# Hybrid decoder layer on one core: the mixer's sums of squares taken with the squares as the stationary operand, and kept on chip until the group's root

## The chip, the cores and the metric

The kernel runs on one core of one Trainium2 chip. The metric is the device time of one execution in microseconds (us), lower is better. A core has five engines that run their own instruction streams and meet through semaphores: TensorE (PE in the profile, with its weight loads shown apart as PEld), VectorE (DVE), ScalarE (ACT), GpSimd (POOL) and SyncE (SP), which here only issues DMAs.

## The reference

A layer norm of x (1024 rows of 1024), one large input projection, two token mixers in parallel, a gated merge, an output projection and a second layer norm. The change lies in the state-space mixer's gated group norm:

```
def gated_group_rmsnorm(y, z, g):
    h = (y * jax.nn.silu(z)).astype(jnp.float32)
    hg = h.reshape(*h.shape[:-1], SSM_GROUPS, -1)
    hg = hg * lax.rsqrt(jnp.mean(jnp.square(hg), axis=-1, keepdims=True) + RMS_EPS)
    return (hg.reshape(h.shape) * g).astype(y.dtype)
```

There are 4 groups of 512 channels and 1024 rows of sequence, so the norm needs 4 x 1024 means of squares, and of each its reciprocal root.

## The kernel before

The input projection is cut into 44 pairs of column tiles of the weights (`pairs`). A pair is seven products (`item_p`, lines 945 to 947 issue the matmuls: 4 blocks of k, each with 3 matmuls of 512 columns). Products of the pairs follow one another on PE without a break. ACT copies every weight block into a rounded form (`whip`, line 276), DVE forms the rest (`wlop`, line 106), POOL forms sums of weight blocks (`s`, `raw_a`: lines 236 to 250). Tiles `pU`, `p`, `oa`, `ob` are the products' PSUM banks and their sums in SBUF.

Between the products the state-space mixer is worked off in small stages (`micro`, one list of stages for each of 4 groups x 8 chunks of 128 rows of the sequence = 32 chunks, numbered n = 8g + c). One entry of the list is issued after each item of the projection, so the order on every engine is the order in which the program is written (`pin`). A chunk ends so: `s_gate_z` forms y * silu(z), `s_square` squares it (ACT, tile `z`, 128 channels x 4 x 128 rows), `s_fold` adds the four channel blocks on POOL, and `s_sum` lets PE add the 128 channels. PE takes two operands: the stationary one, which is loaded into the array first (a row LDWEIGHTS on PEld), and the moving one, which is streamed through it (a row MATMUL). A matmul of f32 is two such passes; a transpose is one.

Before the change `s_sum` has a column of ones as stationary operand (128 x 1) and the squares as moving operand (128 x 128); the result is one row of 128 sums on one partition. ACT scales the row into SBUF (tile `row`) and issues a DMA into DRAM (`ssq_d`). After a group's eighth chunk (`group_rstd`) POOL loads the 1024 sums back as 128 x 8 (`ms`), ACT and DVE form the reciprocal root (`rsqrt`: tiles `rqa`, `rqb`, `rr`), and POOL writes it to `rst_d`. From there `prep_y` (line 784) reads it much later as rows spread over all partitions.

The DMAs that POOL issues are written by POOL itself; those of SP and ACT go through a queue of their own engine.

Of the kernel before, what the change touches and what calls it, by code (L numbers as in the profile page):

```python
# [19 lines left out]
F32 = mybir.dt.float32  # L20
F32R = mybir.dt.float32r
AF = mybir.ActivationFunctionType
# [3 lines left out]
P = 128  # L26
L = 1024
# [3 lines left out]
NCH = 8  # L31
H = 32
G = 4
# [12 lines left out]
def trunk_kernel(ctx: ExitStack, tc: tile.TileContext, x, w_in, w_dt, w_a, w_s, w_o, par, con,  # L46
                 dt_bias, a_log, ln_in_g, ln_in_b, ln_g, ln_b, out):
    nc = tc.nc
    V, S, Gp, PE, SP = nc.vector, nc.scalar, nc.gpsimd, nc.tensor, nc.sync
# [7 lines left out]
    bc_d = [tc.dram_tile([P, 2, L], F32, name=f"bc_d{g}") for g in range(G)]  # L57
    cum_d = tc.dram_tile([H, L], F32, name="cum_d")
    ecum_d = tc.dram_tile([H, L], F32, name="ecum_d")
    ssq_d = [tc.dram_tile([1, L], F32, name=f"ssq_d{g}") for g in range(G)]  # L60
    rst_d = [tc.dram_tile([1, L], F32, name=f"rst_d{g}") for g in range(G)]

    cst = ctx.enter_context(tc.tile_pool(name="cst", bufs=1))
# [3 lines left out]
    ident, upper, slow, ones = (con_t[:, i * P:(i + 1) * P] for i in range(4))  # L67
# [17 lines left out]
    def rsqrt(pool, r, v, n, tag):  # L85

        ve = pool.tile([P, n], F32, tag=tag + "a", name=tag + "a")
        q = pool.tile([P, n], F32, tag=tag + "b", name=tag + "b")
        S.activation(q, v, AF.Sqrt, bias=eps_t, scale=1.0)
        V.tensor_scalar(ve, v, EPS, -0.5, ALU.add, ALU.mult)  # L90
        V.reciprocal(r, q)
        if n == 1:
            V.scalar_tensor_tensor(q, r, ve, r, ALU.mult, ALU.mult)
        else:
            V.tensor_tensor(q, r, r, ALU.mult)
            V.tensor_tensor(q, q, ve, ALU.mult)
        V.scalar_tensor_tensor(r, q, 1.5, r, ALU.add, ALU.mult)
# [55 lines left out]
    def bank(tag, name):  # L153
        return pa.tile([P, HALF], F32, tag=tag, name=name, bufs={"U": 2, "yy": 2}.get(tag, 1))
# [414 lines left out]
    sd = {}  # L569
    XT, ZS, BC, EM, YT, XD, XW, CB, BS, ST = ({} for _ in range(10))  # L570

    def srows(g, c):
        return slice(c * P, (c + 1) * P)
# [131 lines left out]
    def s_store(n):  # L705
        g, c = divmod(n, NCH)
        SP.dma_start(gat_d[g][:, :, srows(g, c)], YT[n])

    def s_sum(n):
        g, c = divmod(n, NCH)  # L710
        ps = bank("tr", f"trs{n}")
        PE.matmul(ps[0:1, 256:384], lhsT=ones[:, 0:1], rhs=ZS[n][:, 0, :], start=True, stop=True)
        row = sd["p"].tile([1, P], F32, tag="row", name=f"row{n}", bufs=1)
        S.activation(row, ps[0:1, 256:384], AF.Copy, scale=1.0 / 512.0)
        S.dma_start(ssq_d[g][:, srows(g, c)], row)
        if c == NCH - 1:
            group_rstd(g)

    def group_rstd(g):
        ms = cst.tile([P, NCH], F32, tag="ms", name=f"ms{g}")  # L720
        Gp.dma_start(ms, ssq_d[g].squeeze(0).rearrange("(p c) -> p c", c=NCH))
        r = cst.tile([P, NCH], F32, tag="rr", name=f"rr{g}")
        rsqrt(cst, r, ms, NCH, "rq")
        Gp.dma_start(rst_d[g].squeeze(0).rearrange("(p c) -> p c", c=NCH), r)

    NS = G * NCH
    micro = []
# [13 lines left out]
    for n in range(NS):  # L741
        stage((s_main, n), (s_decay, n + 1, 0), (s_load_z, n))
        stage((s_rows, n), (s_decay, n + 1, 1), (s_load, n + 2))
        stage((s_gate, n))
        stage((s_turn, n + 1, 0), (s_gate_z, n), (s_load_y, n + 1))
        stage((s_turn, n + 1, 1), (s_square, n), (s_state, n), (s_load_x, n + 2))
        stage((s_mask, n + 1), (s_weigh, n + 1), (s_fold, n))
        stage((s_sum, n), (s_store, n))
# [427 lines left out]
```

## Time and profile before

| what | value |
|---|---|
| median of 3 runs | 1457.02 us (1455.95 to 1457.52) |
| the profiled execution | 1455.73 us, its span 1454.0 us |
| mean granted clock of TensorE | 0.989 of full speed |
| busy: PE, PEld, DVE, ACT, POOL | 96%, 76%, 70%, 49%, 33% of the span |
| DMA | 217.02 MB, mean 149 GB/s |

The span runs from the first to the last instruction of the profile, 1.7 us less than the time of that execution. PE is the engine that is nearly always busy; but a share over the whole span is an average, and what a change in one place is worth is read there: by the starts of successive rows on PE, and by what ended each wait.

### The profile page before, as it was taken

To read this page: it belongs to the slowest core of one execution; us is meant where nothing else is said; L and a number is where in the kernel's file an instruction comes from. 1 tells how busy PE (TensorE), PEld (TensorE's weight loads), DVE (VectorE), ACT (ScalarE), POOL (GpSimd) and SP (SyncE) were. 2 spreads that over 40 slices of the span, in tenths; PEclk is the share of its full clock that TensorE was granted. 3 is DMA by queue.
4 is the path that set the end of the run, shared out by engine and by line. 5 is a ranking of instruction groups with operands and counts; after the bars stand their busy time and mean duration, and the time that the engine had idled before them with its cause. 6 is when DMAs were issued, how large, how long until landed. Compare 5 with 4: busy or idle time off the path is not lost.

```text
span 1454.0 us, 18639 instructions
## 1 busy us (share of the span) xinstructions
PE 1396.3 (96%) x6522; PEld 1102.6 (76%) x6522; DVE 1022.1 (70%) x1495; ACT 716.0 (49%) x1243; POOL 481.0 (33%) x374
## 2 busy tenths in 40 slices
PE   6999999999999999999999999999899999959997
PEld 4677878787777878777878878787678888847786
DVE  7957878877788787787887585776534338778763
ACT  3664556555665655575645656555621233112321
POOL 4012334535244444335453344444000004331054
PEclk9999999999999999999999999999999999989999
DMA  6022354454454454454734545544547736567331
GB/s 231 16 109 80 112 144 128 137 159 133 142 130 136 138 155 123 137 131 135 172 118 134 161 125 150 151 124 138 218 162 242 232 118 218 213 212 288 131 127 62
DMA packets 171901, 217.02 MB, mean 149 GB/s; under 512 B 11520, under 2 KB 116896, under 8 KB 171808
## 3 DMA queue, kind: packets, MB, share of 16 engines
q1 hardware_dynamic: 162128, 181.80, 42.2%
q10 hardware_dynamic: 8272, 29.81, 5.2%
q0 software_dynamic: 1408, 4.23, 0.7%
q8 instruction: 51, 0.84, 0.2%
q14 instruction: 42, 0.34, 0.1%
HBM read 160.97 MB, written 54.82 MB: 148 GB/s over the span
## 4 chain that ended last, share of the span: by engine, by line
PE 80%; DVE 10%; DMA 5%; ACT 3%; issue 2%; ACTq 0%; SPq 0%; POOL 0%; POOLq 0%; DVEq 0%
PE p L945 10%; PE p L947 10%; PE p L946 10%; PE pU L947 8%; PE pU L945 8%; PE pU L946 8%; DMA yg<-yag_d 3%; PE ya L659 2%; PE p_ws L800 2%; PE p_ws L802 2%; PE p_ws L801 2%; PE p_wa L802 2%; PE p_wa L801 2%; PE p_wa L800 2%; PE st L664 2%
## 5 line engine op out<-in xcount | busy, mean ns | idle before, releaser
L106 DVE TENSOR_TENSOR wlop<-raw_a,whip 128x512 fp32r<-128x512 f32 x210 | 180.8, 861 | 171.4 <-ACT whip L276 66.7
L945 PE MATMUL p<-b,whip 128*128 128x512 f32 x352 | 144.0, 410 | 4.3 <-DVE ob L954 4.3
L945 PE MATMUL pU<-t,whip 128*128 128x512 f32 x352 | 144.7, 412 | 3.0 <-ACT oa L980 3.0
L276 ACT ACTIVATE whip<-raw_a 128x512 fp32r<-128x512 f32 x210 | 127.6, 622 | 36.9 <-issue 10.5
L945 PE MATMUL p<-t,whip 128*128 128x512 f32 x352 | 141.8, 403 | 1.5 <-DVE oa L954 1.5
L947 PE MATMUL p<-t,wlop 128*128 128x512 f32 x352 | 139.2, 395 | 1.5 <-DVE wlop L106 1.5
L946 PE MATMUL p<-b,whip 128*128 128x512 f32 x352 | 139.9, 398 | 0.0
L947 PE MATMUL p<-b,wlop 128*128 128x512 f32 x352 | 139.7, 397 | 0.0
L947 PE MATMUL pU<-t,wlop 128*128 128x512 f32 x352 | 139.0, 396 | 0.5 <-DVE wlop L106 0.4
L946 PE MATMUL p<-t,whip 128*128 128x512 f32 x352 | 138.9, 395 | 0.0
L946 PE MATMUL pU<-t,whip 128*128 128x512 f32 x352 | 138.9, 395 | 0.0
L644 POOL TENSOR_TENSOR xw<-xd,dte_t 128x256 f32<-128x256 f32 x56 | 47.0, 840 | 259.0 <-DVE xd L630 259.0
L802 PE MATMUL p_ws<-y,wlos 128*128 128x512 f32 x256 | 104.3, 408 | 12.4 <-DVE wlos L106 12.4
L801 PE MATMUL p_ws<-y,whis 128*128 128x512 f32 x256 | 103.9, 406 | 5.2 <-DVE y L106 5.2
L800 PE MATMUL p_ws<-y,whis 128*128 128x512 f32 x256 | 103.6, 405 | 0.0
L236 POOL TENSOR_TENSOR s<-raw_a,raw_a 128x512 f32<-128x512 f32 x42 | 69.5, 1654 | 85.1 <-DVE wlop L106 74.0
L250 POOL TENSOR_TENSOR raw_a<-raw_a,s 128x512 f32<-128x512 f32 x42 | 66.0, 1572 | 95.4 <-issue 87.4
L863 POOL TENSOR_TENSOR rs<-rs,ag 128x1024 f32<-128x1024 f32 x8 | 19.5, 2444 | 231.4 <-ACT rs L862 231.4
L945 PEld LDWEIGHTS p<-b,whip 128*128 128x128 f32 x352 | 66.8, 190 | 27.4 <-issue 8.8
L106 DVE TENSOR_TENSOR wlop<-s,whip 128x512 fp32r<-128x512 f32 x84 | 80.1, 966 | 9.4 <-PE p L947 6.3
L610 ACT ACTIVATE em<-em,cum_t 128x128 f32<-128x128 f32 x256 | 81.3, 390 | 7.3 <-ACT ob L554 4.4
L945 PEld LDWEIGHTS pU<-t,whip 128*128 128x128 f32 x352 | 66.1, 188 | 20.0 <-ACT oa L980 4.3
(223 smaller groups left out, 3353.7 us busy)
## 6 DMA issues: line engine op xcount, KB each, us to landing
raw_a<-in_w_in_dram SPq DMA_DIRECT2D x168, 256.0 KB
em<-cum_d SPq DMA_DIRECT2D x64, 256.0 KB
xg_d<-cv ACTq DMA_DIRECT2D x16, 512.0 KB
xT<-xg_d SPq DMA_DIRECT2D x32, 256.0 KB
z<-zs_d SPq DMA_DIRECT2D x32, 256.0 KB
gat_d<-y SPq DMA_DIRECT2D x32, 256.0 KB
rb<-rst_d SPq DMA_DIRECT2D x16, 512.0 KB
gt<-gat_d SPq DMA_DIRECT2D x16, 512.0 KB
```

Of the source, the lines that this page charges most:

```text
L106: return eng.tensor_tensor(lo, full, hi.bitcast(F32), ALU.subtract)
L236: Gp.tensor_tensor(s1, r["a21"], r["a22"], ALU.add)
L250: Gp.tensor_tensor(a12, a12, s1s[p]["s2"], ALU.subtract)
L276: S.activation(flat(hi), src, AF.Copy)
L610: S.activation(em[:, h, :], em[:, h, :], AF.Relu, bias=cum_t[:, 8 * g + 4 * i + h, c:c + 1], scale=-1.0)
L644: Gp.tensor_tensor(xw, XD[n, i], dte_t[:, hs, c].unsqueeze(2).to_broadcast([P, HG, HD]), ALU.mult)
L800: PE.matmul(ps, lhsT=hi[:, k, :], rhs=u[:, 0, :], start=start, stop=False)
L801: PE.matmul(ps, lhsT=hi[:, k, :], rhs=u[:, 1, :], start=False, stop=False)
L802: PE.matmul(ps, lhsT=lo[:, k, :], rhs=u[:, 0, :], start=False, stop=stop)
L945: PE.matmul(ps, lhsT=hi[:, k, :], rhs=u[:, 0, :], start=first, stop=False, skip_group_check=True)
L946: PE.matmul(ps, lhsT=hi[:, k, :], rhs=u[:, 1, :], start=False, stop=False, skip_group_check=True)
L947: PE.matmul(ps, lhsT=lo[:, k, :], rhs=u[:, 0, :], start=False, stop=(k == 3), skip_group_check=True)
```

## The change

`s_sum` swaps the operands: the squares become the stationary operand (128 x 128), one column of ones the moving one (128 x 1), and the 128 sums come out as a column, one on each partition. ACT scales that column straight into column c of a tile `ms` of 128 x 8. The row, its DMA into DRAM and the load back are gone. The root is formed on `ms` as before, and POOL writes it to `rst_d`. As the element for partition p and chunk c now belongs at position c * 128 + p of the DRAM row, where it was p * 8 + c, the write is of single elements instead of 8 adjoining ones.

```diff
-    ssq_d = [tc.dram_tile([1, L], F32, name=f"ssq_d{g}") for g in range(G)]
...
+    MS = {}
+
     def s_sum(n):
+
         g, c = divmod(n, NCH)
+        if c == 0:
+            MS[g] = cst.tile([P, NCH], F32, tag="ms", name=f"ms{g}")
         ps = bank("tr", f"trs{n}")
-        PE.matmul(ps[0:1, 256:384], lhsT=ones[:, 0:1], rhs=ZS[n][:, 0, :], start=True, stop=True)
-        row = sd["p"].tile([1, P], F32, tag="row", name=f"row{n}", bufs=1)
-        S.activation(row, ps[0:1, 256:384], AF.Copy, scale=1.0 / 512.0)
-        S.dma_start(ssq_d[g][:, srows(g, c)], row)
+        PE.matmul(ps[:, 256:257], lhsT=ZS[n][:, 0, :], rhs=ones[:, 0:1], start=True, stop=True)
+        S.activation(MS[g][:, c:c + 1], ps[:, 256:257], AF.Copy, scale=1.0 / 512.0)
         if c == NCH - 1:
-            group_rstd(g)
-
-    def group_rstd(g):
-        ms = cst.tile([P, NCH], F32, tag="ms", name=f"ms{g}")
-        Gp.dma_start(ms, ssq_d[g].squeeze(0).rearrange("(p c) -> p c", c=NCH))
-        r = cst.tile([P, NCH], F32, tag="rr", name=f"rr{g}")
-        rsqrt(cst, r, ms, NCH, "rq")
-        Gp.dma_start(rst_d[g].squeeze(0).rearrange("(p c) -> p c", c=NCH), r)
+            r = cst.tile([P, NCH], F32, tag="rr", name=f"rr{g}")
+            rsqrt(cst, r, MS[g], NCH, "rq")
+            Gp.dma_start(rst_d[g].squeeze(0).rearrange("(c p) -> p c", p=P), r)
```

On ACT, at the last chunk of group 0, the order before was this (`oa`, `whip` and `cv` belong to the projection; a table load fetches the function that the next ACTIVATE needs):

```order
L276 ACTIVATE whip_5_3769<-s_17_3674 128x512
L714 ACTIVATE row_3788<-trs_3786 1x128
L715 DMA ssq_d_115<-row_3788 1x128
L89 ACT_TABLE_LOAD
L89 ACTIVATE rqb<-ms_3791,eps_t 128x8
L276 ACTIVATE whip_7_3813<-raw_a_3572 128x512
```

On ACT at the same place the order is now this (line numbers are those of the changed kernel):

```order
L275 ACTIVATE whip_5_3752<-s_17_3657 128x512
L717 ACTIVATE ms_2063<-trs_3769 128x1
L88 ACT_TABLE_LOAD
L88 ACTIVATE rqb<-ms_2063,eps_t 128x8
L275 ACTIVATE whip_7_3792<-raw_a_3555 128x512
```

The DMA is gone from ACT's stream, and the root's first step reads what ACT itself wrote two instructions earlier.

On POOL, at the same place, the order before was this (`z` are the squares being folded, `raw_a` and `s` the weight sums of the next pairs):

```order
L702 TENSOR_TENSOR z_3615<-z_3615 128x256
L703 TENSOR_TENSOR z_3615<-z_3615 128x128
L721 DMA ms_3791<-ssq_d_115 128x8
L724 DMA rst_d_119<-rr_3793 128x8
L250 TENSOR_TENSOR raw_a_3570<-raw_a_3570,s_17_3675 128x512
L236 TENSOR_TENSOR s_18_3910<-raw_a_3808,raw_a_3810 128x512
```

On POOL at the same place the order is now this:

```order
L701 TENSOR_TENSOR z_3598<-z_3598 128x256
L702 TENSOR_TENSOR z_3598<-z_3598 128x128
L721 DMA rst_d_115<-rr_3772 128x8x1
L249 TENSOR_TENSOR raw_a_3553<-raw_a_3553,s_17_3658 128x512
L235 TENSOR_TENSOR s_18_3889<-raw_a_3787,raw_a_3789 128x512
```

One DMA is gone, and the other one has single elements as its innermost pieces. On PE and DVE nothing moved: the sum stands where it stood, between the same matmuls of the projection, with its shape turned from 1x128 to 128x1.

## Rows read from the trace of the kernel before

**Rows 1.** The page, its first line.

```profile
span 1454.0 us, 18639 instructions
```

**Rows 2.** Busy time by stretch: start:end, length, engines (instructions), PEclk, DMA share, GB/s.

```profile
235.00:421.00 186.00, 186.00 (x929) 148.16 (x928) 142.75 (x201) 108.03 (x197) 77.19 (x64) 1.00 0.49 138
...
1033.00:1061.40 28.40, 19.70 (x75) 14.45 (x75) 16.70 (x31) 17.77 (x30) 2.42 (x3) 0.94 0.53 193
```

**Rows 3.** Timeline of PE around the first sum: start us, us, line, operation.

```profile
234.74 0.40 PE L946 MATMUL p<-b,whip 128*128 128x512 f32 x1
234.97 0.39 PE L947 MATMUL p<-b,wlop 128*128 128x512 f32 x1
235.29 0.38 PE L712 MATMUL trs<-z,con_t 128*1 128x128 f32 x2
...
235.95 0.39 PE L946 MATMUL p<-b,whip 128*128 128x512 f32 x1
```

**Rows 4.** Timeline of PE around five short passes of the mixer.

```profile
273.51 0.39 PE L947 MATMUL pU<-t,wlop 128*128 128x512 f32 x1
273.74 0.38 PE L618 MATMUL tr<-con_t,xT 128*128 128x128 f32 x2
273.95 0.27 PE L622 MATMUL tr<-con_t,bc 128*128 128x128 f32 x1
274.06 0.39 PE L623 MATMUL tr<-bc 128*128 128x128 f32 x2
...
274.53 0.39 PE L946 MATMUL p<-t,whip 128*128 128x512 f32 x1
```

**Rows 5.** Groups by form: xcount | busy us, mean ns of one | idle before.

```profile
L623 PE MATMUL tr<-bc 128*128 128x128 f32 x64 | 12.4, 275 | 0.0
...
L623 PEld LDWEIGHTS tr<-bc 128*128 128x128 f32 x64 | 9.7, 191 | 0.0
L712 PEld LDWEIGHTS trs<-z,con_t 128*1 128x1 f32 x64 | 2.8, 81 | 11.7 <-issue 5.5 <-POOL raw_a L250 4.4 <-POOL z L703 1.8
```

**Rows 6.** The chain that ended last, at the end of group 0.

```profile
421.33 0.28 ACT row L714
...
421.62 2.00 DMA ssq_d<-row
...
424.20 2.13 DMA ms<-ssq_d
```

**Rows 7.** All waits of the engines: us in total, times, longest.

```profile
DVE rqa L90 <- DMA ms<-ssq_d: 17.1, 4, 7.1
```

**Rows 8.** Waits of PE from 421 to 868, the ends of groups 0 to 2.

```profile
PE tr L618 <- DVE xd L630: 2.9, 3, 1.0
PE pU L945 <- ACT oa L980: 1.4, 2, 1.0
PE pU L947 <- DVE wlop L106: 0.4, 2, 0.2
```

**Rows 9.** Timeline of ACT at the end of group 3.

```profile
1033.41 0.27 ACT L714 ACTIVATE row<-trs 1x128 f32<-1x128 f32 x1 [1.99 <-PE trs L712]
...
1033.98 1.28 ACT L89 ACT_TABLE_LOAD   x1 [0.30 <-ACT row L714]
1038.19 0.30 ACT L89 ACTIVATE rqb<-ms,eps_t 128x8 f32<-128x8 f32 x1 [2.92 <-DMA ms<-ssq_d]
```

**Rows 10.** Waits of PE from 1033 to 1061.4, the longest of four.

```profile
PE p L945 <- DVE ob L954: 4.1, 1, 4.1
```

**Rows 11.** Instructions on the tile rst_d: ns min/median/max, first and last start.

```profile
L784 SPq DMA_DIRECT2D rb<-rst_d x16: 319/326/517, 1067.0 to 1277.9; - x16
L724 POOL DMA_DIRECT2D rst_d<-rr x4: 540/540/546, 427.8 to 1039.6; - x4
```

**Rows 12.** Timeline of POOL after the root of group 0.

```profile
428.36 1.31 POOL L250 TENSOR_TENSOR raw_a<-raw_a,s 128x512 f32<-128x512 f32 x1
```

**Rows 13.** Timeline of ACT at the copy that reads POOL's result of rows 12.

```profile
437.94 1.13 ACT L276 ACTIVATE whip<-raw_a 128x512 fp32r<-128x512 f32 x2
```

## The prediction

> **What bounds the kernel now.** I read the profile in three steps. First, busy time by stretch, cut at the ends of the four groups of the mixer: from 235 to 421 us PE is busy for all of the 186.00 us at a granted clock of 1.00, and the other three stretches between group ends look the same [rows 2]. There PE sets the time, and what is taken out of its stream comes out of the total. At the group ends it doesn't: from 1033 to 1061.4 PE is busy for 19.70 of 28.40 us, at a clock of 0.94 [rows 2]. Second, PE's own timeline at the place of the sum, where successive starts tell what the sum costs. Third, at the group ends, the waits and the chain, to see what the other engines are late for.
>
> **The sum on PE.** In the projection a matmul starts every 0.23 us. From the start of the last matmul before the first sum (234.97) to the second one behind it (235.95) there are 0.98 us, where two steps would take 0.47; so the sum costs PE 0.51 us [rows 3], although it streams only 2 x 128 columns. The reader should look at where this goes: the sum's load of one column is short (81 ns), but before it PEld idles for 11.7 us over 32 sums, 0.37 us each [rows 5]. Loads elsewhere run beside the matmul in front of them. This one, for an array of 128 x 1 in place of 128 x 128, begins only when the stream has run out, and the next matmul pays again on the way back.
>
> The form that comes in has 128 x 128 as its stationary operand, like its neighbours. The trace has five short passes of that form in a row: two transposes, one more, and an f32 matmul of two passes. From 273.51 to 274.53 are 1.02 us, less 0.47 gives 0.55 us, so 0.11 us a pass, and PEld does not idle before the f32 one [rows 4, 5]. These passes stream 128 columns where the new one streams one. If the stream set the 0.11 us, the new one would be cheaper; if the load of 128 columns does, it is the same. The lower bound is nothing for the stream and one exposed load, some 0.11 us for both passes; the upper bound comes under the rivals. I take the load, 2 x 0.11 = 0.22 us, because the load is what these five passes and the new ones have in common. The saving is 0.51 - 0.22 = 0.29 us, times 32 sums: **9.2 us**, all of it inside or at the edge of stretches where PE never waits.
>
> A rule of the Trainium skill speaks against this. TensorEngine Tiling, section "When to Use Tiling", says that with a short free dimension of the moving operand one should swap stationary and streaming operand and tile the columns, which is the form that this change leaves. By that rule PE would lose, not win; rows 3 and 5 show no gain from the narrow form but a wait around it. What it would take for the rule to be right here is the third rival.
>
> **The end of a group.** After a group's eighth sum, ACT scales the row (421.33, 0.28 us), the DMA to DRAM takes 2.00 us, and the load back, issued by POOL at 424.20, takes 2.13 us [rows 6]. All three lie on the chain that ended last. Behind them wait DVE (17.1 us over the four ends, the longest 7.1 us) [rows 7] and ACT (2.92 us at the last end [rows 9]). Both run their streams in order: behind DVE's first step of the root stand `wlop` and the sums of `p`, behind ACT's stand `whip` and the copies of `pU`, and PE waits for these a few microseconds later.
>
> With the change ACT writes `ms` itself. At the last end the row is done at 1033.41 + 0.27 = 1033.68; the table load of 1.28 us can follow at once, so the root begins near 1034.98 in place of 1038.19 [rows 9]: 3.2 us earlier. At the ends of groups 0 to 2 DVE waits 17.1 - 7.1 = 10.0 us for the load, 3.3 us each [rows 7]; that much, less what ACT's table load leaves, goes.
>
> What PE gets of it: at the ends of groups 0 to 2 it waits seven times, 2.9 + 1.4 + 0.4 = 4.7 us, for DVE or ACT, and in none of the undisturbed stretches [rows 8, 2]. A matmul's row lasts 0.39 us though the next one starts after 0.23 [rows 3], so each wait hides 0.16 us more: 4.7 + 7 x 0.16 = 5.8 us, or 1.9 us an end. The other engines come about 3 us earlier than before, more than PE has to make up, so I count all of it: **5.8 us**. At the last end PE's longest wait alone is 4.1 us [rows 10] and DVE and ACT work almost without a break behind the root, so they set the end; it comes earlier by what they start earlier: **3.2 us**. Further waits of PE remain there, since the work of the eight `ya` tiles on ACT and DVE is not touched.
>
> **What costs nothing, and its cover.** ACT loses 32 DMA issues and its copy has another shape; it waited 1.99 us for PE before that copy [rows 9], so neither counts. The write to `rst_d` now has 1024 single elements in place of 128 runs of 8. On POOL it took 0.54 us before [rows 11]. The new price isn't in the trace: from below it is the same 0.54 us; from above, if POOL's time goes by pieces, 8 x 0.54 = 4.3 us. I take the 4.3 us. POOL can begin it about 3 us earlier than the old one at 427.8, at 424.8, so its next instruction, at 428.36 before [rows 12], comes at 429.1, 0.7 us late. The cover: that result was ready at 429.67 and ACT reads it in the second of two copies that begin at 437.94, at about 438.5 [rows 12, 13], so 8.8 us, or 5.7 when ACT is 3.1 us earlier. Together with the 3.6 us from 424.8 to 428.4, POOL may be held 9.3 us before anybody waits. Whoever reads `rst_d` comes at 1067.0 at the earliest [rows 11], after the last write; how long the small pieces take to land matters to nobody.
>
> **Sum.** 9.2 + 5.8 + 3.2 = 18.2 us. The profiled execution took 1455.73 us, 1.7 us more than its span of 1454.0 [rows 1]; that gives 1437.5 us. The median of the runs stands 1.3 us above that execution, so I forecast **1439 us**.
>
> **The rivals.**
>
> *The waits are only exchanged* (1448 us). The write of 1024 elements holds POOL past its cover of 9.3 us, over 9 ns an element, or the backlog of DVE at a group end is its own work, and PE waits as before. Then only the sum's 9.2 us come out: 1455.7 - 9.2 + 1.3 = 1448. Against it: the chain runs through both DMAs [rows 6], and the root's start is the one thing that both late engines share. The Trainium skill, DMA: Bandwidth & Descriptors, section "Rules for kernel authors", says that a non-contiguous last dimension becomes one descriptor per element and should be avoided. It gives no price for POOL, and no row of this kernel shows one.
>
> *The sum costs PE what it did* (1448 us). If the wait around the sum were for the folded squares and not for the array, it would stay: the idle rows name POOL for 6.2 of the 11.7 us [rows 5]. Then only 5.8 + 3.2 = 9.0 us come out: also 1448. Against it: the wait is alike with either releaser, and the way back to the projection pays too, for which no such data are due.
>
> *The swap is a loss* (1461 us). This ends on the other side. If the two loads of 128 columns and the two one-column passes ran one behind the other, at the full length of their rows, the sum would cost 2 x (0.191 + 0.275) = 0.93 us [rows 5], 0.42 more than now, 13.4 us in all. With the 9.0 us of the group ends: 1455.7 + 13.4 - 9.0 + 1.3 = 1461. It decides from 0.79 us a sum on, where 32 x 0.28 eats the 9.0 us. For it: with one column to stream there is nothing behind which the second load can hide. Against it: five passes of that form with as short a stream take 0.11 us each [rows 4]. This is also what the rule of TensorEngine Tiling would come to.
>
> *More than forecast* (1434 us). The exposed load is paid once (0.11 us for both passes: 3.5 us more), and the clock holds at the last end, where 0.06 of 28.4 us is 1.7 us.
>
> **How the numbers follow.** The forecast has 0.69 (its own range 1436 to 1444, for group ends that give back 5 us less or the clock's 1.7 us more); waits exchanged 0.12; sum no cheaper 0.06; more than forecast 0.06; a loss 0.05, and 0.02 for no change, a smaller loss on PE that the group ends just pay. The range from 1433 to 1449 takes in all but the last two and a little of the tails, about 0.85. A measurement of this kernel can tell 0.2%, 2.9 us, from no change: faster 0.93, same 0.02, slower 0.05.
>
> **What would show it.** Right: PE's starts around the sum leave 0.22 us beyond two steps, and PEld doesn't idle before its load; no DMA stands between the sum and the root; the table load is followed by the root without a wait; PE's waits at the ends of groups 0 to 2 are gone and the long one near 1057 is shorter by 3 us; POOL's write to `rst_d` takes at most 9 us. Wrong: the sum costs over 0.4 us, or the projection waits for `raw_a` or `s` from POOL behind that write.

## The result

The changed kernel takes 1442.98 us (median of 5 runs, 1441.42 to 1443.94), the kernel before in the same comparison 1457.12 us (1455.95 to 1457.59): a ratio of 0.990, 95% interval 0.989 to 0.992. It is 14.1 us faster. The forecast was 1439 us with a range of 1433 to 1449. The profiled execution took 1443.94 us, the longest of the five, and its span is 1441.9 us, 12.1 us less than that of [rows 1].

**The sum.** The timeline of PE around the first sum of the changed kernel, which answers to [rows 3]:

```profile
236.00 0.39 PE L944 MATMUL p<-b,wlop 128*128 128x512 f32 x1
236.23 0.28 PE L716 MATMUL trs<-con_t,z 128*128 128x1 f32 x2
236.37 0.48 PE L942 MATMUL p<-b,whip 128*128 128x512 f32 x1
236.69 0.40 PE L943 MATMUL p<-b,whip 128*128 128x512 f32 x1
```

From 236.00 to 236.69 are 0.69 us, less two steps (0.47) leaves 0.22 us, where 0.51 stood. The groups by form (busy us, mean ns of one | idle before), which answer to [rows 5]:

```profile
L716 PEld LDWEIGHTS trs<-con_t,z 128*128 128x128 f32 x64 | 11.7, 188 | 3.5 <-POOL z L702 1.0
L716 PE MATMUL trs<-con_t,z 128*128 128x1 f32 x64 | 9.2, 213 | 0.0
```

The load got longer (188 ns for 81), and PEld idles 3.5 us before the 32 sums instead of 11.7, that is 0.11 us each instead of 0.37.

**The ends of groups 0 to 2, and the last one.** All waits of PE, first from 415 to 868 us (answering to [rows 8]), then from 1005 to 1065 (answering to [rows 10]); us in total, times, longest:

```profile
PE tr L617 <- DVE xd L629: 0.2, 1, 0.2
...
PE p L942 <- DVE ob L951: 7.7, 1, 7.7
PE p L944 <- DVE wlop L105: 1.5, 1, 1.5
```

The waits at the ends of groups 0 to 2 are gone but for 0.2 us. At the last end, the kernel before had these beside its wait of 4.1 us:

```profile
PE pU L945 <- ACT oa L980: 1.6, 1, 1.6
PE p L945 <- DVE oa L954: 1.5, 1, 1.5
PE p L947 <- DVE wlop L106: 1.5, 1, 1.5
```

Two of the three went, but the long one grew from 4.1 to 7.7 us. The root is not to blame. ACT's timeline, which answers to [rows 9]:

```profile
1020.01 0.17 ACT L717 ACTIVATE ms<-trs 128x1 f32<-128x1 f32 x1 [1.80 <-PE trs L716]
1020.20 1.28 ACT L88 ACT_TABLE_LOAD   x1
1021.50 0.30 ACT L88 ACTIVATE rqb<-ms,eps_t 128x8 f32<-128x8 f32 x1
...
1038.47 0.63 ACT L275 ACTIVATE whia<-raw_a 128x512 fp32r<-128x512 f32 x1 [3.79 <-DMA raw_a<-in_w_a_dram]
```

The root's first step follows 1.3 us after the sum's copy with nothing between but the table load. What is late comes 17 us later: ACT waits 3.79 us for a load of weights. The chain that ended last, from there to PE:

```profile
1027.33 0.32 SPq L754
1027.69 10.70 DMA raw_a<-in_w_a_dram
1038.47 0.63 ACT whia L275
...
1043.23 0.61 DVE ob L951
1043.98 0.77 PE p L942
```

Before, no load of `raw_a` stood on this stretch of the chain. Here one takes 10.70 us. The instructions of SP on that tile from 1015 to 1045 us (ns min/median/max) say that one issue alone took 5.6 us:

```profile
L224 SPq DMA_DIRECT2D raw_a<-in_w_a_dram x8: 328/428/5611, 1027.7 to 1040.4; - x8
```

The DMA view from 1020 to 1040 us shows all that the queues did meanwhile. The first line has 40 slices of 0.5 us; then one queue (ACT's: in this stretch it issues only the two stores `sgs_d`) with packets, MB and share of 16 engines' time; then issues, KB each, and the median us from issue to landing. A packet counts in the slice in which it starts:

```profile
GB/s 254 98 213 344 393 41 25 41 0 8 33 180 344 0 8 8 8 16 0 0 0 41 0 0 8 16 25 82 361 336 385 320 234 328 401 434 389 397 410 410
...
q10 hardware_dynamic: 288, 1.05, 51.3%
...
sgs_d<-oa ACTq DMA_DIRECT2D x1, 512.0 KB, 10.6
sgs_d<-ob ACTq DMA_DIRECT2D x1, 512.0 KB, 10.4
```

From slice 14 to 27, 1026.5 to 1033.5 us, next to nothing is started, while loads and stores are queued: this is called the hole below. ACT's 288 packets took 51.3% of 16 engines over 20 us, 164 us or 0.57 us each. In the kernel before, the same view of the 20 us behind its last sum reads:

```profile
q10 hardware_dynamic: 290, 1.05, 13.0%
```

That is 42 us, 0.14 us each. By the packet records of the two traces the means differ through a few packets: in the changed kernel 25 of the 288 last over 1 us, up to 7.5, and make 121 of the 164 us, while the median is 0.16 us in both; in the kernel before none lasts 1 us. What POOL issued ahead of the hole is the write of the root to `rst_d` (at 1022.9), answering to [rows 11]:

```profile
L721 POOL DMA_DIRECT2D rst_d<-rr x4: 924/928/1082, 423.8 to 1022.9; - x4
...
DMA to landing us min/median/max: 3.3/5.2/16.8
```

Two narrower DMA views tell where that write stands. From 1024 to 1026 us (first line) all 32 packets of POOL's queue q0 start; from 1026 to 1034 (second line) ACT's q10 is the only queue that starts any:

```profile
q0 software_dynamic: 32, 0.00, 24.2%
...
q10 hardware_dynamic: 68, 0.28, 104.4%
```

So the engines are through with the write's own packets before the hole begins. What fills all 16 engines in the hole are 68 packets of ACT's stores, at 2.0 us each (1.044 x 16 x 8 / 68; some reach beyond the window, hence over 100%), and SP's loads start none.

The prediction had said of this write that how long the small pieces take to land matters to nobody. The theory to be tested: **1024 single elements, written side by side, hold up the packets of every other queue for some 7 us, and at the last end loads that PE needs are among them.** "Side by side" is meant in DRAM: there the neighbours come from neighbouring partitions, while the 8 elements of one partition lie 512 bytes apart. Its rivals: the earlier root has only moved DVE's and ACT's backlog, or the loads now start at a worse moment.

### The profile page after: what moved, and what is told of

It is laid out like the page before. It is cut to its first block, busy times and chain, and to the rows that moved or that the text cites. A ratio compares the mean times of both kernels' runs of the same rounds, so it can differ in the third digit from the quotient of the medians.

```text
span 1441.9 us, 18560 instructions
## 1 busy us (share of the span) xinstructions
PE 1387.5 (96%) x6522; PEld 1111.4 (77%) x6522; DVE 1027.6 (71%) x1495; ACT 711.4 (49%) x1243; POOL 481.3 (33%) x370
## 4 chain that ended last, share of the span: by engine, by line
PE 82%; DVE 10%; DMA 4%; ACT 2%; issue 1%; ACTq 0%; POOL 0%; SPq 0%; POOLq 0%; DVEq 0%
PE p L942 11%; PE p L944 10%; PE p L943 10%; PE pU L942 8%; PE pU L944 8%; PE pU L943 8%; PE ya L658 2%; PE p_ws L798 2%; DMA yg<-yag_d 2%; PE p_ws L799 2%; PE p_ws L797 2%; PE p_wa L799 2%; PE p_wa L798 2%; PE p_wa L797 2%; PE st L663 2%; PE yb L653 2%
## 5 line engine op out<-in xcount | busy, mean ns | idle before, releaser
L977 ACT ACTIVATE oa<-pU 128x512 f32<-128x512 f32 x41 | 24.6, 600 | 118.8 <-PE pU L944 118.8
```

## The experiments

All times are medians, all ratios are to the kernel before in the same comparison. That kernel's own median goes from 1457.12 to 1457.97 us over the comparisons, so a difference between two rows of the table is uncertain by about that much; the last four columns are read from each kernel's own rows. The last four columns are worked out from the starts of PE's rows in one profiled execution of each: what the sum costs PE (as above, median of 32), first sum to last, the gaps between the last sum of a group and the first of the next (groups 0, 1, 2), and the last sum to the first product of the output projection (`p_wa`).

| kernel | us | ratio, interval | a sum | first to last sum | ends 0, 1, 2 | last end |
|---|---|---|---|---|---|---|
| before | 1457.12 | 1 | 0.51 | 797.70 | 25.70, 25.32, 24.59 | 28.55 |
| changed | 1442.98 | 0.9902, 0.9888 to 0.9915 | 0.22 | 783.46 | 23.07, 23.02, 22.68 | 29.42 |
| e1 wide ones | 1451.02 | 0.9958, 0.9946 to 0.9971 | 0.22 | 789.74 | 25.38, 25.32, 24.41 | 29.45 |
| e2 runs of 8 | 1439.51 | 0.9875, 0.9861 to 0.9888 | 0.22 | 782.73 | 22.68, 22.69, 22.68 | 25.98 |
| e3 row on chip | 1452.90 | 0.9966, 0.9954 to 0.9979 | 0.51 | 791.04 | 23.03, 22.97, 22.95 | 30.15 |
| e4 write twice | 1452.51 | 0.9967, 0.9955 to 0.9980 | 0.22 | 783.79 | 23.18, 23.24, 22.68 | 37.80 |
| e5 turned root | 1440.20 | 0.9878, 0.9862 to 0.9893 | 0.22 | 783.45 | 23.22, 22.79, 22.79 | 25.78 |
| e6 second write 512 B apart | 1445.05 | 0.9910, 0.9897 to 0.9924 | 0.22 | 783.75 | 23.18, 23.23, 22.67 | 30.84 |
| e7 before, single elements | 1463.25 | 1.0036, 1.0024 to 1.0049 | 0.51 | 799.23 | 26.15, 25.72, 25.29 | 32.99 |
| e8 64 B apart | 1445.51 | 0.9914, 0.9897 to 0.9931 | 0.22 | 783.75 | 23.17, 23.23, 22.68 | 30.75 |
| e9 16 B apart | 1445.10 | 0.9914, 0.9899 to 0.9928 | 0.22 | 783.80 | 23.18, 23.24, 22.71 | 30.54 |
| e10 only 16 B apart | 1441.09 | 0.9888, 0.9871 to 0.9904 | 0.22 | 784.76 | 23.60, 23.56, 22.91 | 25.98 |

**e1: the kernel before with all 128 columns of ones as stationary operand.** It separates the width of the loaded operand from the swap.

```diff
-        PE.matmul(ps[0:1, 256:384], lhsT=ones[:, 0:1], rhs=ZS[n][:, 0, :], start=True, stop=True)
+        PE.matmul(ps[:, 256:384], lhsT=ones, rhs=ZS[n][:, 0, :], start=True, stop=True)
```

> The kernel before, with one edit: the stationary operand of the sum is all 128 columns of ones in place of one, so that 128 equal rows come out, of which ACT takes the first as before. The squares are still streamed (128 columns), and the way through DRAM stays. Theory (a stationary operand of another width than its neighbours' makes PE run out before and behind the sum): the sum costs 0.22 us in place of 0.51, PEld's idle time before it goes from 0.37 us to nothing, and the time falls by 32 x 0.28 = 9 us to 1448 us, with PE's waits at the group ends as before. Rival (what counts is which operand is streamed, or that the folded squares come late): the sum still costs 0.5 us and the time stays at 1457 us.

The timeline of PE around its first sum:

```profile
235.90 0.39 PE L947 MATMUL p<-b,wlop 128*128 128x512 f32 x1
236.13 0.38 PE L712 MATMUL trs<-z,con_t 128*128 128x128 f32 x2
236.27 0.48 PE L945 MATMUL p<-b,whip 128*128 128x512 f32 x1
236.59 0.39 PE L946 MATMUL p<-b,whip 128*128 128x512 f32 x1
```

Again 0.69 us less 0.47, so 0.22 us, with operands not swapped and 128 columns streamed. PEld idles before the load as it does in the changed kernel:

```profile
L712 PEld LDWEIGHTS trs<-z,con_t 128*128 128x128 f32 x64 | 11.8, 188 | 3.5 <-POOL z L703 0.9
```

The width of the stationary operand alone makes the 0.29 us, and streaming 128 columns or one makes no difference. The time misses the 1448 expected: against the kernel before beside it 6.8 us came out, 8.0 between the first and the last sum, less what the last end lost. The ends 0 to 2 stayed as they were, since the two DMAs are still there. The last end is 0.9 us longer than before though nothing there was changed: behind the same wait of 4.1 us, 11 steps of PE's matmuls took 0.43 us where before 6 did; the granted clock in that stretch of e1 (1050.1 to 1055.4 us) was 0.50, the lower of the two levels.

**e2: the changed kernel with the root written in runs of 8 adjoining elements,** in the order p * 8 + c, which is not the order in which it is read back.

```diff
-            Gp.dma_start(rst_d[g].squeeze(0).rearrange("(c p) -> p c", p=P), r)
+            Gp.dma_start(rst_d[g].squeeze(0).rearrange("(p c) -> p c", c=NCH), r)
```

> The changed kernel, with one edit: the root is written to DRAM in runs of 8 adjoining elements as before the change, not in single elements. The roots then stand in another order, so the norm uses the wrong row's root; nothing else differs. Theory (the write of 1024 single elements holds up the DMAs behind it, and at the last group end the loads of w_a come late for that): SP's issue of 5.6 us there goes, the loads land in about 6 us, PE's longest wait falls from 7.7 us to about 4, and the time falls by 3 to 4 us to 1439 or 1440 us. Rival (the last end is set by the work of ACT and DVE on the eight ya tiles whenever it starts): within 1 us of 1443 us.

The last end becomes 25.98 us, 3.4 less than in the changed kernel, and the total 1439.5. Its DMA view from 1020 to 1040 us:

```profile
GB/s 90 205 385 361 8 16 4 5 0 33 295 385 328 25 16 164 221 319 385 365 291 229 90 94 139 377 414 401 418 410 393 410 447 406 328 324 348 303 328 393
...
q10 hardware_dynamic: 288, 1.05, 13.0%
...
sgs_d<-oa ACTq DMA_DIRECT2D x1, 512.0 KB, 3.4
```

The hole behind 1026.5 us is 1 us wide instead of 7, ACT's packets take their 13.0% again (none lasts 1 us), and its first store lands after 3.4 us, not 10.6. PE's longest wait is back at its old length:

```profile
PE p L942 <- DVE ob L951: 4.1, 1, 4.1
```

**e3: the changed kernel with the sum in its old form** (a column of ones stationary); ACT keeps 8 of the 128 sums as a row on chip, and the root is formed on a tile of other data.

```diff
+    ms_t = cst.tile([P, NCH], F32, name="ms_t")
+    V.memset(ms_t, 1.0)
...
-            MS[g] = cst.tile([P, NCH], F32, tag="ms", name=f"ms{g}")
+            MS[g] = ms_t
...
-        PE.matmul(ps[:, 256:257], lhsT=ZS[n][:, 0, :], rhs=ones[:, 0:1], start=True, stop=True)
-        S.activation(MS[g][:, c:c + 1], ps[:, 256:257], AF.Copy, scale=1.0 / 512.0)
+        PE.matmul(ps[0:1, 256:384], lhsT=ones[:, 0:1], rhs=ZS[n][:, 0, :], start=True, stop=True)
+        S.activation(MS[g][0:1, :], ps[0:1, 256:256 + NCH], AF.Copy, scale=1.0 / 512.0)
```

> The changed kernel, but PE takes the sum in the form of before (one column of ones stationary, the squares streamed); ACT copies only eight sums of the row into the tile that the root is formed from, and nothing goes through DRAM. The norm is left out by this: the roots are of ones and of a few sums. Theory: the group ends are those of the changed kernel, and the 32 sums cost 0.51 us again, so the time is 32 x 0.28 = 9 us above the changed kernel: 1452 us. Rival (most of the gain was in the group ends and the sum's price is hidden elsewhere): 1443 to 1446 us.

It is 9.9 us slower than the changed kernel by the medians, 9.2 when each is set against the kernel before in its own comparison. Of that PE's rows show 7.4 us in the 28 gaps between the sums inside the groups, which is the sums' share there, and 0.7 at the last end. The single elements are still written here, and ACT's packets take 50.4% in the same view (1026 to 1046 us). Against the kernel before, its three group ends are together 6.7 us shorter and its last end is 1.6 us longer, 5.1 in all; measured are 4.9 (1457.84 in that comparison).

**e4: the changed kernel with a second write of the root,** side by side as the first, to a scratch row in DRAM.

```diff
+    again_d = [tc.dram_tile([1, L], F32, name=f"again_d{g}") for g in range(G)]
...
             Gp.dma_start(rst_d[g].squeeze(0).rearrange("(c p) -> p c", p=P), r)
+            Gp.dma_start(again_d[g].squeeze(0).rearrange("(c p) -> p c", p=P), r)
```

> The changed kernel with the write of the root done twice, the second time into a DRAM tile that nobody reads, also in 1024 single elements. Theory (single elements hold up the DMAs behind them by some 8 us a write): the stall at the last group end doubles, SP's or ACT's DMAs there take up to 16 us, and the time rises by 5 to 9 us to 1448 to 1452 us; POOL's issue takes 0.93 us more. Rival (the slow loads at the last end have another cause): within 1 us of 1443 us.

The last end grows by another 8.4 us and the total by 9.5. Its DMA view from 1021 to 1041 us and its longest wait of PE:

```profile
q10 hardware_dynamic: 73, 0.30, 80.9%
```

```profile
PE p L944 <- DVE ob L953: 16.0, 1, 16.0
```

Only 73 of ACT's 288 packets start in these 20 us, at 3.5 us each (0.809 x 16 x 20 / 73). The dose points at the write, and not at the moment at which the loads start. That it isn't POOL's time for a second write either, e6 shows.

**e5: the changed kernel with the root turned on PE** into 8 x 128 and written as 8 rows of 512 bytes by ACT's queue.

```diff
+    def turn_root(g, r):
+        ps = bank("tr", f"trr{g}")
+        PE.transpose(ps[0:NCH, 0:P], r, ident)
+        rt = sd["p" if g < G - 1 else "x"].tile([NCH, P], F32, tag="rt", name=f"rt{g}")
+        S.activation(rt, ps[0:NCH, 0:P], AF.Copy)
+        S.dma_start(rst_d[g].squeeze(0).rearrange("(c p) -> c p", p=P), rt)
...
-            Gp.dma_start(rst_d[g].squeeze(0).rearrange("(c p) -> p c", p=P), r)
+            later.setdefault(now[0] + 2, []).append(lambda: turn_root(g, r))
```

> The changed kernel, but the root of 128 x 8 is turned on PE into 8 x 128 (one transpose a group, two items later), copied by ACT and written to DRAM as 8 rows of 512 bytes by ACT's queue, so no write of single elements is left. If the 1024 single elements of the last group hold up the loads and stores beside them for some 8 us, and the kernel loses about 3.5 us by it at its last end: 1439 to 1440 us, the last sum to the first weight product of the output projection about 26 us as with runs of 8, where the changed kernel has 29.4. The turn itself should cost PE about 0.2 us a group. If the delay comes from POOL's own time in the write or from where the last end stands: 1443 us, 29 us.

1440.2 us, the last end 25.78. It forms the same norm as the changed kernel and beats both kernels: the interval of its ratio ends at 0.9893, the changed kernel's begins at 0.9888 with its middle at 0.9902, so against the latter the lead of 2.8 us is likely, not beyond doubt. The last end itself is 3.6 us shorter. PE's waits at the last end:

```profile
PE p L949 <- DVE ob L958: 2.6, 1, 2.6
PE p L951 <- DVE wlop L105: 2.1, 1, 2.1
```

**e6, e8, e9: the second write of e4, but each element 512, 64 or 16 bytes from the next** (s = 128, 16 or 4 elements of scratch for each one written). They ask whether the number of pieces or their neighbourhood costs. The edit of e6:

```diff
+    far_d = [tc.dram_tile([1, 128 * L], F32, name=f"far_d{g}") for g in range(G)]
...
+            Gp.dma_start(far_d[g].squeeze(0).rearrange("(c p s) -> p c s", p=P, c=NCH)[:, :, 0], r)
```

> The changed kernel with a second write of the same 1024 roots into scratch memory, again as single elements, but each 512 bytes from the next, so that no two of them share a line of DRAM. If the number of small pieces is what holds the other queues up, this costs the same as the second write of adjoining elements did: about 1452 us, some 38 us from the last sum to the first product of the output projection. If it is that many pieces fall on the same piece of DRAM (1024 partial writes into 4 KB), the second write costs little: 1443 to 1446 us, 29 to 32 us.

> The changed kernel with a second write of single elements as before, but 64 bytes from one another. With 512 bytes between them the second write cost 1.4 us at the last end, adjoining 8.4 us. If what slows the pieces is that several of them fall into the same 64 bytes: as with 512 bytes, about 31 us from the last sum to the first product of the output projection, 1445 us. If it is that they fall into the same few KB: nearer to 37 us, 1451 us.

> The same with 16 bytes from one element to the next, so that four share 64 bytes, where sixteen do in the adjoining write. If the cost goes by how many share 64 bytes: between the two, about 32 to 33 us from the last sum, 1446 to 1448 us. If each piece that shares its 64 bytes with any other costs the same: 37 us, 1451 us. If only spans shorter than 16 bytes matter: 31 us, 1445 us.

The same 1024 pieces cost 1.4, 1.3 and 1.1 us at the last end where adjoining ones cost 8.4. Pieces 16 bytes apart cost no more than those 512 apart. Of e9's three expectations the last one came true (31 us, 1445 us), and the graded one did not. As POOL issues two writes in all of these, its time is not what makes the 8.4.

**e7: the kernel before with one edit, its write as single elements.**

```diff
-        Gp.dma_start(rst_d[g].squeeze(0).rearrange("(p c) -> p c", c=NCH), r)
+        Gp.dma_start(rst_d[g].squeeze(0).rearrange("(c p) -> p c", p=P), r)
```

> The kernel before with one edit: its write of the roots to DRAM is of single elements (the roots come to stand in another order, so the norm is of other rows). If this write alone costs what the change lost at its last end: slower, by 4 to 8 us (1461 to 1465 us), nearly all between the last sum and the first product of the output projection (28.6 us before), since the write comes some 3 us later here and meets the same loads. If the loss needs the new form of the sums or the earlier root: no change, 1457 us.

5.3 us slower (1457.97 in that comparison), 4.4 of them at the last end. The chain there now runs through a load of weights, and PE's longest wait goes from 4.1 to 7.9 us:

```profile
1045.89 10.95 DMA raw_a<-in_w_a_dram
...
1061.69 0.61 DVE ob L954
1062.43 0.76 PE p L945
```

```profile
PE p L945 <- DVE ob L954: 7.9, 1, 7.9
```

So neither the new form of the sum nor the earlier root is needed for the loss.

**e10: e2 with a write of single elements 16 bytes apart beside it,** the only single elements left.

```diff
+    far_d = [tc.dram_tile([1, 4 * L], F32, name=f"far_d{g}") for g in range(G)]
...
-            Gp.dma_start(rst_d[g].squeeze(0).rearrange("(c p) -> p c", p=P), r)
+            Gp.dma_start(rst_d[g].squeeze(0).rearrange("(p c) -> p c", c=NCH), r)
+            Gp.dma_start(far_d[g].squeeze(0).rearrange("(c p s) -> p c s", p=P, c=NCH)[:, :, 0], r)
```

> The changed kernel with its roots written in runs of 8 (another order, so the norm is of other rows), and beside it a write of the same 1024 roots as single elements 16 bytes from one another into scratch memory: the only write of single elements left. If pieces that stand apart cost little by themselves: 1439 to 1441 us, 26 to 27.5 us from the last sum to the first product of the output projection. If 1024 single elements cost some 3.5 us wherever they land, and the second one of the runs before only hid behind the first: 1443 us, 29 to 30 us.

The last end is that of e2, 25.98 us. Its DMA view from 1020 to 1040 us:

```profile
q10 hardware_dynamic: 288, 1.05, 16.3%
...
far_d<-rr POOLq DMA_DIRECT2D x1, 4.0 KB, 4.5
```

16.3% instead of 51.3%, and the write lands after 4.5 us. By the packet records the spaced elements occupy the engines as long as the adjoining ones do (0.41 to 0.49 us for 15 of its 16 packets of 256 bytes, 0.03 in runs of 8); it is the stores behind them that are not held up. The 1.6 us that it takes more than e2 lie at the ends of groups 0 to 2, 2.0 us longer together. There (415 to 868 us) PE waits again for DVE, which it doesn't in e2:

```profile
PE tr L618 <- DVE xd L630: 1.4, 2, 0.7
```

So the spaced write is free at the last end only; why DVE comes late at the others stays open.

## Why the prediction was right, and which step of it was not

**The sum: right.** Forecast were 0.22 us and 9.2 us in all. Between the group ends, the 28 gaps from one sum to the next became 722.09 / 28 - 714.69 / 28 = 0.264 us shorter (first to last, less the three ends), 8.5 us for 32. e3 gives 9.2 with the run's spread in it. Of load and stream as what sets the 0.11 us of a pass, e1 rules out the stream: with 128 columns streamed and with one, the sum costs the same. That it is the load, and not some fixed price of a pass, no run shows. One sign was a little off: PEld idles 0.11 us before each sum, where nothing was expected. The rival of 1461 us, with a sum of 0.93 us, falls. The prediction had set a rule of the Trainium skill beside it, the swap in TensorEngine Tiling (Array Packing), "When to Use Tiling"; for a single sum among these neighbours the swapped form is the dearer one (0.51 us, 0.22 in the other), and packing several tiles into the array was not tried. The same page of the Trainium skill says under "Key Properties" that a change of tiling mode drains TensorE. The 0.29 us for the way there and back would fit that; whether a stationary operand of 128 x 1 counts as another mode, no run here shows.

**The ends of groups 0 to 2: right.** Forecast 5.8 us; the three ends are together 6.84 us shorter, less 3 x 0.26 for the sums in them, 6.1 us (6.8 in e2, without the single elements). ACT's stores are held up there too: in the DMA view from 424 to 444 us the first line is the changed kernel's, the second e2's.

```profile
q10 hardware_dynamic: 144, 0.52, 43.6%
...
q10 hardware_dynamic: 144, 0.52, 6.4%
```

That PE hardly waits there all the same is where these ends differ from the last one, at which loads that PE needs stand behind the stores. The rival in which the waits are only exchanged falls: PE waits 0.2 us at these three ends.

**The price on POOL: right that it doesn't matter.** The write took POOL 0.93 us, not the 4.3 assumed: eight times the pieces took 1.7 times as long.

**The last end: the step that failed.** The prediction counted 3.2 us there; measured were 0.9 us the other way, 4.1 us short of the sum, and that is the distance from 1439 to 1443. PE's starts show the sizes. The three short gaps of 1.90, 1.96 and 1.90 us (start to start, so with the step of 0.23 inside and what the matmul's pipeline hides) became two of 0.50 and 1.88 and a plain step of 0.23: 3.2 us won. The long one grew from 4.51 to 8.07: 3.6 lost. Behind it 10 steps of 0.43 us stand for 6: 0.8 lost. With the 0.3 that the last sum saves, the balance is the 0.9 lost that was measured.

The wrong sentence was that "how long the small pieces take to land matters to nobody". It asked who reads `rst_d`, and not who shares the DMA engines with the write. Without the single elements (e2) the long gap is 4.51 again. There the step's mechanism holds: counted from the last sum, PE's product behind the long wait starts 20.7 us later, before 24.1, so DVE and ACT do end 3.4 us earlier because they start earlier. But even there the long wait is not 3 us shorter, as the list of signs had it. PE arrives earlier too, since its short waits shrink, and the wait keeps its 4.1 us. And behind it 12 steps of 0.43 us stand for 6, which takes 0.8 us that the sum had no term for. So e2's 1439.5 meets the forecast to 0.5 us partly by luck: its first three ends give 1.0 us more than counted and its last one 0.9 less (2.6, of which the sum itself is 0.3).

The prediction had named the page that warns of such writes (the Trainium skill, DMA: Bandwidth & Descriptors, "Rules for kernel authors") but looked for a price on POOL alone. The price is real, 3.4 us at the last end here, though e10 shows that at this end it is not the number of elements that is paid for.

**What stays open.** Why adjoining single elements slow the stores behind them, and ones 16 bytes apart don't. The same page of the Trainium skill says under "Specifications" that below 512 bytes a transfer is a read, a change and a write; by that sentence alone the pieces of e9 and e10 should cost what those of e4 do, and they don't. Distance and extent are not told apart: 1024 adjoining elements also fall into one stretch of 4 KB, 16 bytes apart they spread over 16 KB. Distances of 8 bytes, a write of adjoining elements spread over several such stretches, and a write by fewer DMA engines were not tried. The profiled execution of the changed kernel also has 0.9 us more from PE's first matmul to its first sum, and 0.8 more from its first `p_wa` to PE's last end, than that of before; over all runs the former goes from 226.6 to 228.0 us with no order in it, so it is taken as spread.

## What to carry to other kernels

Keep the stationary operand of a stray matmul as wide as its neighbours': among matmuls of 128 x 128, one column of ones cost 0.29 us more than 128 of them. When a result goes out in single elements, ask who else has DMAs in flight in the next 10 us, stores above all, not only who reads it; turn it on chip into rows first (one transpose), or at least don't let the pieces adjoin in DRAM (here only a scratch write was spaced so; what reading such rows back costs was not measured). And where a chain ends in a wait for a weight load, look at the queue of the other engine's stores too: its packets' mean time (share x engines x time / packets) tells a held-up DMA engine from a late issue. It doesn't name the culprit: here it was a write whose own packets were already over.

## What the chip showed that was not expected

4 KB in 1024 adjoining single elements took the packets of another queue from 0.14 to 0.57 us in the mean, and a second such write to 3.5 us; the write's own packets were over before, and single packets of the stores behind it lasted up to 7.5 us; one issue on SP took 5.6 us meanwhile, where the median is 0.43. The same 4 KB with 16 bytes from element to element left them at 0.18 us (16.3%). And after a wait of 4.1 us, the same length in the kernel before, e1, e2 and e10, PE's steps stayed at 0.43 us for 6, 11, 12 and 13 matmuls, where a step at full clock is 0.23: in the stretch behind that wait in e2 the granted clock was 0.50, the lower of the two levels:

```profile
1039.80:1045.20 5.40, 5.40 (x13) 4.24 (x14) 1.03 (x2) 0.30 (x1) 0.00 (x0) 0.50 0.13 53
```
